# Activations that TensorE holds stationary: the two token halves laid out in turn, and read with a step of two elements

## The chip, the cores and the metric

The kernel runs on one core of a Trainium2 chip. A core has five engines with queues of their own: TensorE (PE, matrix products), VectorE (DVE), ScalarE (ACT), GpSimd (POOL) and SyncE (SP, which issues most transfers). A matrix product on TensorE is two records in the profile: a weight load, which puts a 128x128 stationary block into the array (row PEld), and the matmul proper, which streams a moving block of up to 512 columns past it (row PE). The metric is the device time of one execution in microseconds, lower is better.

## What is computed

One decoder layer on 256 tokens of width 2048, in float32. Cut to the products and what joins them:

```python
proj = x @ w_in                                   # q/k/v/gates of two branches
o = gla_chunked(q, k, v, log_a)                   # gated linear attention, 4 heads
y_gla = o @ w_branch_gla
y_fox = fox_attention(fqh, fkh, fvh, log_f) @ w_branch_fox
mix = (sigmoid(ma) * y_gla + sigmoid(mb) * y_fox) @ w_out
x = layer_norm(ALPHA * x + mix, ln1_g, ln1_b)
h = gelu(causal_dwconv(x @ w_gate, conv_w, conv_b)) * (x @ w_up)
x = layer_norm(ALPHA * x + h @ w_down, ln2_g, ln2_b)
x = x + sigmoid(x @ w_ple_gate) * (p @ w_ple_proj)
```

D_MODEL is 2048 and D_FF 5632, so the weights are 309 MB and each is used once.

## The kernel before

**High and low parts.** Each float32 operand is split into a high part, rounded to the type fp32r by a ScalarE copy, and a low part, the VectorE difference of the operand and its high part. A product is then three fp32r products: high by high, high by low, low by high.

**Which operand is stationary.** There are two kinds of product. In the first (`w_unit` L300, `w_phase` L315) the weights are stationary and the activations move past them, high and low parts of all 256 tokens in one moving block of 512 columns; this serves q, k, the gate and up projections. In the second the activations are stationary, one block of 128 features by 128 tokens at a time, and 512 weight columns move: the value projection (L472), the merge gates and the two branch projections (`q_unit`, L979, called psm, psa and psb), the v and gate projections of the linear attention, the output and down projections and half of the last gate (`s_half`, L841: gv, gr, wo, dn, pg), and the rest (`x_mm`, L353: pg, pp). L909 is the last quarter of pg in 256-column pieces. A block of tokens is one half t of the 256. Every one of these matmuls loads its stationary block anew, also where it is the same as the one before.

**Seven products.** In `s_half` most pairs of weight blocks go through Strassen's scheme, seven products in place of eight. Its sums of activation blocks are made by `s_sums` (L791) on VectorE, split, and kept as cells of 256 columns, high part in columns 0 to 127 and low part in 128 to 255 (`cell`, L787).

**Layout.** An activation tile holds for each block of 128 features a row of 512 columns: the high part of tokens 0 to 127, of tokens 128 to 255, then the low parts in the same order. So a stationary block is always 128 neighbouring columns, `a[:, t * P:t * P + P]`. Tiles of this kind are xT, oT, ofT, mC, x1T, hC, x2T, pTs; mS, xS, hS and gS hold cells. x1T is the only one that is moving alone.

**What sets the order.** Weights arrive in units of 1 MB on SP's queue; `prep` and `prep_s` split them three units ahead of use (L241, L215 with copies at L121). The order on the other engines is set by a scheduler from the order in the code and priorities; TensorE, the bound engine, runs strictly in that order. Some weight differences of the Strassen pairs are made early, parked in memory (POOL's queue) and read back (SP's), both named td.

Of the kernel before, what the change touches and what calls it, by code (L numbers as in the profile page):

```python
# [78 lines left out]
def tile_block(ctx: ExitStack, tc: tile.TileContext, wu, wfv, wpp, xT_in, x_in, pT_in, wlr,  # L79
# [37 lines left out]
    def mxtile(name):  # L117
        return pmx.tile([P, 512], F32, tag="mx", name=name)

# [209 lines left out]
    def comb(ps, o, scale=1.0):  # L329
        tmp = t1("tmp")  # L330
        copy(tmp, ps[:, 256:512], scale)
        a = ps[:, 0:256]
        if len(o.shape) == 3:
            a, tmp = [v.rearrange("p (t n) -> p t n", t=2) for v in (a, tmp)]
# [123 lines left out]
    for u in range(8):  # L458
        hi, lo = fvu[u]
        for j in range(2):  # L460
            kt = 2 * u + j
            a = xT[kt // 4][:, kt % 4, :]
            prods = [[(hi[j], a[:, t * P:t * P + P]), (hi[j], a[:, 256 + t * P:256 + t * P + P]),
                      (lo[j], a[:, t * P:t * P + P])] for t in range(2)]
# [119 lines left out]
    def fox_gen():  # L584
# [40 lines left out]
        def values(h):  # L625
# [7 lines left out]
            copy(dst[:, 0:256], po[:, 0:256])  # L633
            nc.vector.tensor_tensor(dst[:, 256:512], po[:, 0:256],
                                    dst[:, 0:256].bitcast(F32), ALU.subtract)
# [16 lines left out]
    for n in range(16):  # L652
# [8 lines left out]
        comb(ps, fqk[h // 4][:, h % 4, j], (P ** -0.5, 1.0)[j])  # L661
# [137 lines left out]

    def sums(y, name, scale=1.0, full=False):  # L800
# [7 lines left out]
        for e, src in parts:  # L808
            copy(o[:, e, 0:P], src, scale)
            hi = o[:, e, 0:P].bitcast(F32)  # L810
            if scale == 1.0:
                nc.vector.tensor_tensor(o[:, e, P:256], src, hi, ALU.subtract)
            else:
                nc.vector.scalar_tensor_tensor(o[:, e, P:256], src, scale, hi, ALU.mult,
# [111 lines left out]
    def x_sums(pairs):  # L926
        for i, pair in pairs:
# [20 lines left out]
            v = s_sums(y)  # L948
            for j, w in enumerate(ws):
                src = v[:, j * m:j * m + m]  # L950
                copy(w[:, :, 0:P], src)
                nc.vector.tensor_tensor(w[:, :, P:256], src, w[:, :, 0:P].bitcast(F32),
                                        ALU.subtract)
            yield

    def x_cl(pair, j, t):
        kt = 2 * pair + j
        a = xT[kt // 4][:, kt % 4, :]
        return a[:, t * P:t * P + P], a[:, 256 + t * P:256 + t * P + P]

    def x_st(pair, i):
        if i < 3:
            return x_cl(pair, (0, 1, 1)[i], (0, 0, 1)[i])
        o = xS[pair][i - 3]
        return o[:, 0:P], o[:, P:256]


    def q_unit(ps, act, k, first, last, tick=None):
# [4 lines left out]
        def part(i, t):  # L973
            kt = 4 * k + i
            o = act[kt // 4][:, kt % 4, :]
            ah, al = o[:, t * P:t * P + P], o[:, 256 + t * P:256 + t * P + P]
# [139 lines left out]
    def split_T(pt, dst, t):  # L1116

        p3 = pt.rearrange("p (k t) -> p k t", t=P)
        hi = dst[:, :, t * P:t * P + P]
        copy(hi, p3)  # L1120
        nc.vector.tensor_tensor(dst[:, :, 256 + t * P:256 + t * P + P], p3,
                                hi.bitcast(F32), ALU.subtract)
# [19 lines left out]
    def turn_pair(pair):  # L1142
# [19 lines left out]
        nc.vector.scalar_tensor_tensor(dst[:, :, 256:512], p3, 0.5,  # L1162
                                       dst[:, :, 0:256].bitcast(F32), ALU.mult, ALU.subtract)
# [24 lines left out]
    def ln_steps(zof, stats, t, act_out, gb_, cg, cb, nm, prio, aff):  # L1188
# [29 lines left out]
        def turn(g):  # L1218
            zc = zof(t, g)
            with tc.high_priority(prio):  # L1220
# [3 lines left out]
                if g in aff:  # L1224
                    split_T(pt, act_out[g], t)
                    return
                y = t2("lny").rearrange("p (k t) -> p k t", t=P)
                for i in range(4):
# [5 lines left out]
                    else:  # L1234
                        nc.vector.tensor_scalar(y[:, i, :], src, gc, bc, ALU.mult, ALU.add)
                hi = act_out[g][:, :, t * P:t * P + P]
                copy(hi, y)
                nc.vector.tensor_tensor(act_out[g][:, :, 256 + t * P:256 + t * P + P], y,
                                        hi.bitcast(F32), ALU.subtract)
# [3 lines left out]
    def out_proj(nh, tail, mid, end=None):  # L1243
        def cl(pair, j, t):
# [4 lines left out]
            return a[:, t * P:t * P + P], a[:, 256 + t * P:256 + t * P + P]  # L1249
# [170 lines left out]
    for n in range(NF):  # L1420
# [31 lines left out]
        copy(dst[:, 0:256], h)  # L1452
        nc.vector.tensor_tensor(dst[:, 256:512], h, dst[:, 0:256].bitcast(F32), ALU.subtract)
        if pair in DN_S[0] and j == 1:
            v = s_sums(yp)
            for i in range(2):
                w = sm.tile([P, 2, 256], F32R, tag="t2", bufs=6, name="hs")
                copy(w[:, :, 0:P], v[:, 2 * i:2 * i + 2])
                nc.vector.tensor_tensor(w[:, :, P:256], v[:, 2 * i:2 * i + 2],
                                        w[:, :, 0:P].bitcast(F32), ALU.subtract)  # L1460
# [27 lines left out]
    def down(nh, tail, mid):  # L1488
        def cl(pair, j, t):
            a = hC[pair // 2][:, pair % 2 * 2 + j, :]  # L1490
            return a[:, t * P:t * P + P], a[:, 256 + t * P:256 + t * P + P]
# [107 lines left out]
    def g_cl(pair, j, t):  # L1599
        kt = 2 * pair + j  # L1600
        a = x2T[kt // 4][:, kt % 4, :]
        return a[:, t * P:t * P + P], a[:, 256 + t * P:256 + t * P + P]
# [3 lines left out]
    def g_sums(pairs):  # L1606
        two = s8([P, 8, 256], F32R, name=f"gS{pairs[0]}")
        for i, pair in enumerate(pairs):
# [4 lines left out]
            v = s_sums(y)  # L1613
            copy(o[:, :, 0:P], v)
            nc.vector.tensor_tensor(o[:, :, P:256], v, o[:, :, 0:P].bitcast(F32), ALU.subtract)
# [80 lines left out]

def _chan(v):
# [3 lines left out]
def _layout(i):  # L1701
# [26 lines left out]
    for lev in range(1, 8):  # L1728
# [5 lines left out]
    return dict(wu=wu, wfv=wfv, wpp=_xst(i["w_ple_proj"][0]), xT=x.T.reshape(16, P, S).transpose(1, 0, 2),  # L1734
                x=x.reshape(2, P, D), pT=_fold(i["p"][0, 0]).T.reshape(2, P, S).transpose(1, 0, 2),
# [22 lines left out]
```

## Time and profile before

| | before |
|---|---|
| time, median of 3 runs (lowest to highest) | 1645.58 us (1645.08 to 1645.61) |
| span of the profiled execution | 1645.0 us |
| PE, share of the span, matmuls | 1638.4 us, 100%, 8422 |
| PEld, share | 1404.3 us, 85% |
| DVE, share | 1356.0 us, 82% |
| ACT, share | 910.3 us, 55% |
| DMA | 477.81 MB, mean 290 GB/s |
| granted TensorE clock, mean | 1.000 |

The median of the runs is 0.6 us above the span of the profiled execution, so sums made on the span are carried over by adding 0.6. In the chain of waits a row reads: start in us, length in us, engine, tile and line, and how many instructions were merged. Matmuls are pipelined, so the recorded length of one (389 ns for 512 columns) is longer than the distance from one start to the next; the length of a merged row of the chain divided by its count is that distance.

### The profile page before, as it was taken

How to read it: one execution, taken by the hardware profiler on the slowest of the kernel's cores; microseconds unless marked ns; L12 is line 12 of the kernel's file. 1: busy time of each engine (PE TensorE's matmuls, PEld its weight loads, DVE VectorE, ACT ScalarE, POOL GpSimd, SP SyncE). 2: the span in 40 equal slices, each digit the busy share in tenths (PEclk: the TensorE clock that was granted, in tenths of full speed). 3: DMA queues.
4: the chain of work that ended last, by engine and by line, in shares of the span. 5: the costliest groups of instructions: out<-in, count | busy, mean ns of one | idle time of the engine just before them, and what ended most of it. 6: DMA issues, size and time to landing. Idle time of an engine off the chain costs nothing.

```text
span 1645.0 us, 23490 instructions
## 1 busy us (share of the span) xinstructions
PE 1638.4 (100%) x8422; PEld 1404.3 (85%) x8422; DVE 1356.0 (82%) x1964; ACT 910.3 (55%) x1277; POOL 92.7 (6%) x244
## 2 busy tenths in 40 slices
PE   9999999999999999999999999999999999999998
PEld 9988888888888888887898888888888888888887
DVE  7687899788989867778987888887887778988887
ACT  6655555456666654446574445555455456566554
POOL 0000000000000000000010111110111000000000
PEclk9999999999999999999999999999999999999999
DMA  8799799878888768889855898888766679899574
GB/s 324 281 371 341 290 383 356 294 258 309 306 333 307 252 207 303 305 335 364 296 190 194 315 338 320 308 306 304 279 239 217 210 260 336 305 343 348 177 258 157
DMA packets 114838, 477.81 MB, mean 290 GB/s; under 512 B 13032, under 2 KB 14320, under 8 KB 95136
## 3 DMA queue, kind: packets, MB, share of 16 engines
q1 hardware_dynamic: 105216, 417.57, 70.8%
q0 software_dynamic: 9504, 58.73, 8.9%
q8 instruction: 66, 1.08, 0.2%
q14 instruction: 52, 0.43, 0.1%
HBM read 417.53 MB, written 58.73 MB: 290 GB/s over the span
## 4 chain that ended last, share of the span: by engine, by line
PE 97%; DMA 1%; DVE 1%; ACT 0%; issue 0%; POOL 0%; ACTq 0%
PE psm L979 11%; PE dn L841 10%; PE psu L307 10%; PE psg L307 9%; PE psa L979 5%; PE psu L309 5%; PE psg L309 5%; PE dn_p L841 4%; PE gr L841 3%; PE gv L841 3%; PE fv L472 3%; PE pg L353 3%; PE psb L979 3%; PE wo L841 2%; PE gr_p L841 2%; PE gv_p L841 2%
## 5 line engine op out<-in xcount | busy, mean ns | idle before, releaser
L241 DVE TENSOR_TENSOR lo<-raw,hi 128x1024 fp32r<-128x1024 f32 x456 | 551.1, 1220 | 140.7 <-ACT hi L121 139.4
L121 ACT ACTIVATE hi<-raw 128x1024 fp32r<-128x1024 f32 x456 | 476.6, 1057 | 304.2 <-DMA raw<-in_wu_dram 83.7
L307 PE MATMUL psu<-x1T,hi 128*128 128x512 f32 x688 | 240.4, 392 | 0.0
L307 PE MATMUL psg<-x1T,hi 128*128 128x512 f32 x672 | 234.8, 392 | 0.0
L309 PE MATMUL psu<-x1T,lo 128*128 128x256 f32 x688 | 192.3, 280 | 0.0
L309 PE MATMUL psg<-x1T,lo 128*128 128x256 f32 x672 | 187.8, 280 | 0.0
L979 PE MATMUL psm<-hi,xT 128*128 128x512 f32 x512 | 163.0, 392 | 0.0
L307 PEld LDWEIGHTS psu<-x1T,hi 128*128 128x128 f32 x688 | 129.2, 188 | 27.6
L307 PEld LDWEIGHTS psg<-x1T,hi 128*128 128x128 f32 x672 | 126.2, 188 | 27.0
L309 PEld LDWEIGHTS psu<-x1T,lo 128*128 128x128 f32 x688 | 130.6, 190 | 0.0
L121 ACT ACTIVATE hi_b<-raw 128x512 fp32r<-128x512 f32 x112 | 92.9, 841 | 66.8 <-DMA raw<-in_wu_dram 17.9
L309 PEld LDWEIGHTS psg<-x1T,lo 128*128 128x128 f32 x672 | 127.6, 190 | 0.0
L159 DVE TENSOR_TENSOR td<-td 128x512 f32<-128x512 f32 x172 | 117.6, 684 | 0.9
L215 DVE TENSOR_TENSOR lo_b<-raw,hi_b 128x512 fp32r<-128x512 f32 x112 | 104.9, 952 | 15.9 <-ACT hi_b L121 15.6
L979 PEld LDWEIGHTS psm<-hi,xT 128*128 128x128 f32 x512 | 96.2, 188 | 19.6
L215 DVE TENSOR_TENSOR lo_t<-td,hi_t 128x1024 fp32r<-128x1024 f32 x86 | 101.7, 1219 | 12.7 <-ACT hi_t L121 12.0
L121 ACT ACTIVATE hi_t<-td 128x1024 fp32r<-128x1024 f32 x86 | 88.0, 1053 | 28.9 <-DMA td<-td 15.1
L979 PE MATMUL psm<-lo,xT 128*128 128x512 f32 x256 | 99.8, 390 | 0.0
L841 PE MATMUL dn<-hi,hC 128*128 128x512 f32 x352 | 97.8, 389 | 0.0
L979 PE MATMUL psa<-hi,oT 128*128 128x512 f32 x256 | 81.2, 392 | 0.0
L841 PEld LDWEIGHTS dn<-hi,hC 128*128 128x128 f32 x352 | 66.0, 188 | 13.7
L979 PEld LDWEIGHTS psa<-hi,oT 128*128 128x128 f32 x256 | 48.1, 188 | 10.0
(414 smaller groups left out, 3130.8 us busy)
## 6 DMA issues: line engine op xcount, KB each, us to landing
raw<-in_wu_dram SPq DMA_DIRECT2D x525, 512.0 KB, 6.3
td<-in_wu_dram SPq DMA_DIRECT2D x43, 1024.0 KB, 8.8
td<-td POOLq DMA_DIRECT2D x43, 1024.0 KB, 7.7
td<-td SPq DMA_DIRECT2D x43, 1024.0 KB, 8.3
hS<-sd SPq DMA_DIRECT2D x11, 1024.0 KB, 8.8
raw<-in_wu_dram SPq DMA_DIRECT2D x43, 256.0 KB, 7.7
fvraw<-in_wfv_dram SPq DMA_DIRECT2D x13, 524.0 KB, 6.6
sd<-hs POOLq DMA_DIRECT2D x24, 256.0 KB, 5.6
```

What stands on the lines that cost most here:

```text
L121: return nc.scalar.activation(o, i, AF.Copy, bias=0.0, scale=scale)
L159: sub = lambda o, a, b: nc.vector.tensor_tensor(o, a, b, ALU.subtract)
L215: nc.vector.tensor_tensor(lo, src, hi.bitcast(F32), ALU.subtract)
L241: i = nc.vector.tensor_tensor(lo, raw, hi.bitcast(F32), ALU.subtract)
L307: nc.tensor.matmul(ps, lhsT=hi[i // 8 if hoff == 0 else 0][:, w0 % 1024:w0 % 1024 + P], rhs=a[:, kt % 4, :], start=first and i == 0, stop= ...
L309: nc.tensor.matmul(ps[:, 256:512], lhsT=lo[i // 8 if hoff == 0 else 0][:, w0 % 1024:w0 % 1024 + P], rhs=a[:, kt % 4, 0:256], start=False, ...
L353: nc.tensor.matmul(bs[j][:, 0:m], lhsT=x, rhs=v[:, o:o + m], start=first and i == 0, stop=last and i == 2)
L472: nc.tensor.matmul(fbk[t][c][:, 0:n], lhsT=x, rhs=w[:, o:o + n], start=kt == 0 and i == 0, stop=kt == 15 and i == 2)
L841: nc.tensor.matmul(ps[:, e], lhsT=x, rhs=w, start=k == 1, stop=k == total.get(id(ps), 3 * ns))
L979: nc.tensor.matmul(ps[t], lhsT=x, rhs=v, start=first and i == 0 and j == 0, stop=last and i == 3 and j == 2)
```

## The change

The layout of every activation tile that is used stationary changes so that the two blocks of a pair lie in turn. In the high half of a row, column 2n + t holds token n of half t; in the low half likewise. In a cell of a Strassen sum, column 2n + j holds token n of the high part (j = 0) or the low part (j = 1). A stationary block is then 128 columns with a step of two elements. The host lays x and p out this way (`_mix`); on the chip the copies and differences that write such tiles write with a step of two, and the first level of `s_sums` reads with a step of two where its source is laid out so (`mixed`). x1T keeps its layout. The results of q and k of the second branch and of the first come out with tokens in turn, since xT is their moving operand, and `comb` puts them back in order as it reads them. Weight tiles, also those that are stationary, keep theirs. The names of the helpers and the core of the diff:

```diff
+    def tok(a, s, t):
+        return a.rearrange("p (s n t) -> p s t n", s=2, t=2)[:, s, t, :]
+
+    def by_half(v):
+        return v.rearrange("p (n t) -> p t n", t=2)
...
 # x_mm; q_unit, x_cl, g_cl, out_proj and down read the same way
-            ah = a[:, t * P:t * P + P]
-            al = a[:, 256 + t * P:256 + t * P + P]
+            ah, al = tok(a, 0, t), tok(a, 1, t)
...
     def cell(o, i):
-        return o[:, i, 0:P], o[:, i, P:256]
+        v = o[:, i, :].rearrange("p (n j) -> p j n", j=2)
+        return v[:, 0, :], v[:, 1, :]
...
-    def s_sums(y):
-        a11, a21, a12, a22 = [y[:, k, t * P:t * P + P] for k in range(2) for t in range(2)]
+    def s_sums(y, mixed=False):
+        h = y.rearrange("p k (n t) -> p k t n" if mixed else "p k (t n) -> p k t n", t=2)
+        a11, a21, a12, a22 = [h[:, k, t] for k in range(2) for t in range(2)]
...
 # turn_pair, the tile mC: one copy and one difference for two blocks become one of each per block
-        dst = mC[i // 2][:, i % 2 * 2:i % 2 * 2 + 2, :]
-        copy(dst[:, :, 0:256], p3, 0.5)
-        nc.vector.scalar_tensor_tensor(dst[:, :, 256:512], p3, 0.5,
-                                       dst[:, :, 0:256].bitcast(F32), ALU.mult, ALU.subtract)
+        for k in range(2):
+            dst = mC[i // 2][:, i % 2 * 2 + k, :]
+            hi, lo = by_half(dst[:, 0:256]), by_half(dst[:, 256:512])
+            src = p3[:, k, :].rearrange("p (t n) -> p t n", t=2)
+            copy(hi, src, 0.5)
+            nc.vector.scalar_tensor_tensor(lo, src, 0.5, hi.bitcast(F32), ALU.mult, ALU.subtract)
...
 # the gated product of the MLP, tile hC
-        copy(dst[:, 0:256], h)
-        nc.vector.tensor_tensor(dst[:, 256:512], h, dst[:, 0:256].bitcast(F32), ALU.subtract)
+        hi, lo = by_half(dst[:, 0:256]), by_half(dst[:, 256:512])
+        h3 = h.rearrange("p (t n) -> p t n", t=2)
+        copy(hi, h3)
+        nc.vector.tensor_tensor(lo, h3, hi.bitcast(F32), ALU.subtract)
...
+def _mix(a):
+    return a.reshape(-1, 2, P).transpose(0, 2, 1).reshape(a.shape)
...
-    return dict(... xT=x.T.reshape(16, P, S).transpose(1, 0, 2),
+    return dict(... xT=_mix(x.T).reshape(16, P, S).transpose(1, 0, 2),
```

The number and the order of instructions stay as they were on SP and POOL. On TensorE the count stays, and two products change place in the output projection. There VectorE makes the low parts of mC from the transposed blocks mt, among the splits of weights (lo_b, lo_t). Its rows were:

```order
L215 TENSOR_TENSOR lo_b_6992<-raw_1_6982,hi_b_6991 128x1024
L1162 SCALAR_TENSOR_TENSOR mC_6213<-mt_7027,mC_6213 128x2x256
L1162 SCALAR_TENSOR_TENSOR mC_7039<-mt_7034,mC_7039 128x2x256
L215 TENSOR_TENSOR lo_t_6996<-td_6985,hi_t_6995 128x1024
L215 TENSOR_TENSOR lo_t_7000<-td_6985,hi_t_6999 128x1024
```

In the changed kernel they are:

```order
L223 TENSOR_TENSOR lo_b_6994<-raw_1_6984,hi_b_6993 128x1024
L1185 SCALAR_TENSOR_TENSOR mC_6213<-mt_7029,mC_6213 128x2x128
L1185 SCALAR_TENSOR_TENSOR mC_7043<-mt_7038,mC_7043 128x2x128
L223 TENSOR_TENSOR lo_t_6998<-td_6987,hi_t_6997 128x1024
L223 TENSOR_TENSOR lo_t_7002<-td_6987,hi_t_7001 128x1024
L1185 SCALAR_TENSOR_TENSOR mC_6213<-mt_7029,mC_6213 128x2x128
L1185 SCALAR_TENSOR_TENSOR mC_7043<-mt_7038,mC_7043 128x2x128
```

One instruction over 2x256 columns became two over 2x128 for each of the two blocks, and the second of each now stands behind two splits of weights. (A third block, made earlier, and ScalarE's copies for all three are cut in two likewise.) On TensorE, in the first half of the output projection, the two Strassen products whose PSUM banks were mt's (wo_p_7067 and wo_p_7066) stood before:

```order
L841 MATMUL wo_p_6980<-hi_t_6928,mS_6269 128x512
L841 MATMUL wo_p_7067<-hi_t_6928,mS_6269 128x512
L841 MATMUL wo_p_7067<-lo_t_6929,mS_6269 128x512
L841 MATMUL wo_p_7067<-hi_t_6928,mS_6269 128x512
L841 MATMUL wo_p_7066<-hi_t_6932,mS_6269 128x512
L841 MATMUL wo_p_7066<-lo_t_6933,mS_6269 128x512
L841 MATMUL wo_p_7066<-hi_t_6932,mS_6269 128x512
L841 MATMUL wo_10_6977<-hi_t_6932,mS_6269 128x512
```

In the changed kernel they (now wo_p_7073 and wo_p_7072) stand ten matmuls later:

```order
L856 MATMUL wo_01_6978<-hi_b_6993,mS_6551 128x512
L856 MATMUL wo_p_7073<-hi_t_6930,mS_6271 128x512
L856 MATMUL wo_p_7073<-lo_t_6931,mS_6271 128x512
L856 MATMUL wo_p_7073<-hi_t_6930,mS_6271 128x512
L856 MATMUL wo_p_7072<-hi_t_6934,mS_6271 128x512
L856 MATMUL wo_p_7072<-lo_t_6935,mS_6271 128x512
L856 MATMUL wo_p_7072<-hi_t_6934,mS_6271 128x512
L856 MATMUL wo_01_6978<-lo_b_6994,mS_6551 128x512
```

These six matmuls moved from ahead of the next unit's products to among them; nothing else on TensorE moved.

More of the change, by code (lines that the diff above doesn't have):

```diff
@@ L333, in comb @@
         if len(o.shape) == 3:
-            a, tmp = [v.rearrange("p (t n) -> p t n", t=2) for v in (a, tmp)]
+            a, tmp = by_half(a), by_half(tmp)
         if scale == 1.0:
@@ L462, in tile_block @@
             a = xT[kt // 4][:, kt % 4, :]
-            prods = [[(hi[j], a[:, t * P:t * P + P]), (hi[j], a[:, 256 + t * P:256 + t * P + P]),
-                      (lo[j], a[:, t * P:t * P + P])] for t in range(2)]
+            prods = [[(hi[j], tok(a, 0, t)), (hi[j], tok(a, 1, t)), (lo[j], tok(a, 0, t))]
+                     for t in range(2)]
             if u < 2:
@@ L1114, in o_gen, with put_T, split_T @@
             yield
[L1116 to L1122, printed above, removed]
+    def put_T(src, dst, t, mixed):
+        if mixed:
+            hi, lo = [dst.rearrange("p k (s n t) -> p s t k n", s=2, t=2)[:, i, t] for i in range(2)]
+        else:
+            hi, lo = [dst[:, :, o + t * P:o + t * P + P] for o in (0, 256)]
+        copy(hi, src)
+        nc.vector.tensor_tensor(lo, src, hi.bitcast(F32), ALU.subtract)
+    def split_T(pt, dst, t, mixed=True):
+        put_T(pt.rearrange("p (k t) -> p k t", t=P), dst, t, mixed)
     mixers.append(o_gen())
```

66 lines of the change are left out of this document (34 added, 32 removed).

## The prediction

> **What bounds the kernel now.** First the page: the span, the engines, and the shares of the chain of waits.
>
> ```profile
> span 1645.0 us, 23490 instructions
> PE 1638.4 (100%) x8422; PEld 1404.3 (85%) x8422; DVE 1356.0 (82%) x1964; ACT 910.3 (55%) x1277; POOL 92.7 (6%) x244
> PE 97%; DMA 1%; DVE 1%; ACT 0%; issue 0%; POOL 0%; ACTq 0%
> ```
>
> TensorE is busy all the time and 97% of the chain is its own work, so what changes the time must change the distance from one matmul to the next. That distance is read from merged rows of the chain (start in us, length, tile and line, count):
>
> ```profile
> 605.26 21.76 PE psa L979 x96
> 627.02 10.88 PE psb L979 x48
> 1000.09 0.23 PE psg L307
> 1001.13 0.23 PE psg L307
> ```
>
> With activations stationary, 21.76/96 = 10.88/48 = 226.7 ns for 512 columns, steadily. With weights stationary, three pairs of 512 and 256 columns lie between the last two rows: 1.04/3 = 347 ns for 768 columns. What would the array itself need? The early rows, and two later ones, tell:
>
> ```profile
> 3.93 0.85 PE warm_ps L131 x2
> 4.79 1.92 PE fv L472 x6
> 102.41 0.43 PE po L628 x2
> 553.13 0.87 PE gt L1102 x8
> ```
>
> In the first microseconds the array runs at half its rate: 425 ns for 512 columns and 320 ns for 384 columns, 0.83 ns a column in both and nothing fixed on top. Later a column takes half of that, 0.417 ns, so 512 need 213.3 ns and the measured 226.7 has 13.3 ns on top. The pairs have the same: 347 less 768 x 0.417 = 27, for two. So at full rate each matmul pays a fixed 13.3 ns, at half rate none. po (L628) is a product of plain float32 that takes two passes: 215 ns for 256 columns, 0.84 ns a column, and again only some 2 ns on top. So the tax appears where the moving operand is read at full rate: 2048 bytes of each partition in 213 ns, 9.6 bytes a ns. It disappears where the moving operand is read at 4.8 bytes a ns. It belongs to the reading from SBUF, not to the array. The other thing read at that time is the next stationary block. The transposes gt, one load each, follow each other in 0.87/8 = 109 ns, so a load of 128 columns takes at most 109 ns: 512 bytes, 4.7 bytes a ns.
>
> **The change, part by part.** It removes and adds no matmul. It gives each activation block that is loaded a step of two. How many are these? The matmuls of L841, L979, L472, L353 and L909, in this order (span, busy time, count, clock, DMA):
>
> ```profile
> 0.00:1645.00 1645.00, 504.71 (x2214) 1.00 0.80 290
> 0.00:1645.00 1645.00, 312.26 (x1344) 1.00 0.80 290
> 0.00:1645.00 1645.00, 47.20 (x288) 1.00 0.80 290
> 0.00:1645.00 1645.00, 57.86 (x240) 1.00 0.80 290
> 0.00:1645.00 1645.00, 4.81 (x36) 1.00 0.80 290
> ```
>
> Together 4122 of 8422, and 4122 x 13.3 = 54.8 us of tax that the change can touch. No row shows a stationary block with a step, so its price is bounded from both sides. Lower end: the tax vanishes, -54.8 us. Upper end: the step makes it twice as large, +54.8 us (each load then passes over 1024 bytes where it passed over 512). Which is nearer? At full rate the moving operand passes through SBUF at 9.6 bytes a ns and the load at 4.7, so the one overtakes the other during each load; with a step of two the load passes at 9.4 and the two keep their distance. The one row here where both already go equally fast is po, 4.8 against 4.7, and its tax is 2 ns. I take that row: 13.3 - 2 = 11.3 ns less, x 4122 = 46.6 us. The weak point is that in po the reading also has slack, which alone would explain it; the first six fv, at half rate and with slack too, show no tax either.
>
> Not all of the 46.6 us reaches the end, because other work is close behind TensorE in some stages. The value projection, gv, the output projection and the first half of the down projection (length, then busy time of PE, PEld, DVE, ACT, POOL, clock, DMA share and GB/s):
>
> ```profile
> 4.80:50.00 45.20, 45.20 (x280) 44.89 (x280) 30.54 (x36) 27.39 (x37) 3.60 (x6) 1.00 0.92 342
> 365.00:449.00 84.00, 83.91 (x374) 69.18 (x373) 76.56 (x102) 54.47 (x68) 0.00 (x0) 1.00 0.83 296
> 739.00:824.00 85.00, 84.22 (x377) 68.56 (x376) 79.01 (x96) 51.26 (x58) 1.53 (x2) 1.00 0.88 325
> 1318.00:1432.00 114.00, 114.00 (x508) 94.53 (x508) 97.56 (x110) 66.79 (x73) 0.70 (x2) 1.00 0.85 309
> ```
>
> In the output projection VectorE has 79.0 of 85 us and PE already waits; some 360 matmuls would save 4.1 us, and I count none of it. In gv VectorE has 76.6 of 84, so I count half of 4.0. In the value projection the DMA engines are 92% busy, so half of 3.3. Elsewhere, as in the last row (97.6 of 114, against about 108 after), there is room. Given back: 4.1 + 2.0 + 1.6 = 7.7 us.
>
> The rest of the change costs nothing or little. ScalarE and VectorE now write, and in places read, with a step of two. Their price stands in the trace, because L713 works on pieces of runs from 64 elements down to every second element:
>
> ```profile
> L713 ACT ACTIVATE e<-e x28: 399/418/449, 186.9 to 364.5; 128x256 f32<-128x256 f32 x28
> L1437 ACT ACTIVATE yc<-yc 128x256 f32<-128x256 f32 x44 | 18.3, 416 | 54.8 <-DVE yc L1436 54.8
> L718 DVE TENSOR_TENSOR kq<-gk,e x28: 408/416/426, 188.0 to 365.3; 128x256 f32<-128x256 f32 x28
> L1450 DVE TENSOR_TENSOR yp<-yc,up 128x256 f32<-128x256 f32 x24 | 10.1, 422 | 0.7 <-ACT yc L1437 0.2
> ```
>
> All 28 lie in 399 to 449 ns around the 416 ns of an unbroken copy; on VectorE 408 to 426 against 422. So 0, covered in any case by TensorE; without that cover 30 ns on some 150 copies, 4.5 us. The host's reordering is outside the metric; SP's and POOL's transfers keep count, size and order. In the output projection the split of mC into two frees the mt banks later:
>
> ```profile
> 746.51 1.28 DVE L1162 SCALAR_TENSOR_TENSOR mC<-mt,mC 128x512 fp32r<-128x512 f32 x2
> 747.71 2.35 DVE L215 TENSOR_TENSOR lo_t<-td,hi_t 128x1024 fp32r<-128x1024 f32 x2
> 747.46 0.62 PE L841 MATMUL wo_p<-hi_t,mS 128*128 128x512 f32 x2
> ```
>
> The two products that need these banks started at 747.69, and come ten matmuls later now, at 747.69 + 2.27 = 749.96. The second pair of mC stands behind the two lo_t, which end at about 750.0, and takes two times about 0.42. So the first of the products waits until about 750.4: +0.5 us, with the rest of the stage queued behind it on PE.
>
> Sum: 1645.0 - 46.6 + 7.7 + 0.5 = 1606.6 on the profile's span, and with the 0.6 us by which the median exceeds it, 1607 us.
>
> **The rivals.** *The tax is not the load's* (no change). A fixed bubble at the start of each moving stream, which a reader with slack hides and one at full rate cannot, gives the same rows: 13.3 at full rate, none at half. A step in the stationary block then touches nothing but the 0.5 us above: 1646 us. For it: the tax is the same 13.3 ns for blocks of very different addresses. Against it: nothing in the trace, since no full-rate matmul comes without a load beside it. [...]
>
> *Twice the fetches* (slower). If the load reads pieces of several neighbouring columns and each piece stops the moving stream for a moment, a step of two makes twice as many pieces and the tax 26.7 ns: +54.8 us, all on TensorE, 1700 us. It decides from the first matmul and everywhere alike. For it: the tax is there only when the moving reader has no slack, as with stolen turns. Against it: 13.3 ns for a whole load of 109 ns is little for stolen turns.
>
> *The load at half speed* (slower). If two columns come with one read now and one then, a load takes up to 218 ns. The 512-column matmuls still cover it (226.7), but fv, of 384 and 280 columns at 173.3 and 130 ns, and L909, of 256 at 120, would wait for it: 192 x 44.7 + 96 x 88 + 36 x 98 = 20.6 us, 1666 us. Against it: no row of this trace. [...]
>
> **How the numbers follow.** The tax shrinks, 0.55: 1607, with its own range from 1597 (46.6 saved and little given back) to 1630 (half the tax goes, 27.4, less the part lost in the near-bound stages and somewhat more). No change, 0.20: 1645 to 1647. Load at half speed, 0.10: 1666. Twice the fetches, 0.15: 1700. The range 1597 to 1668 leaves out the last rival and some 0.03 of the first case. A measurement here can tell 0.2%, 3.3 us, from no change. Faster 0.55, same 0.20, slower 0.25, from the same cases.
>
> **What would show it.** Right: the rows of psa and psb in the chain at 48 matmuls in about 10.4 us, the psg pairs unchanged at 347 ns, VectorE's share up, waits of PE in the output projection. No tax of the load's: 10.88 again. Twice the fetches: about 11.5. Half speed: 10.88 in psb but the value projection longer by 17 us. The forecast fails if psb stays at 10.88, or if psb falls and new waits of PE on VectorE or DMA take more than the 7.7 us.

## The result, and the profile after

The changed kernel took 1668.99 us (median of 4 runs, 1668.77 to 1669.46), the kernel before 1645.33 us (4 runs, 1644.32 to 1645.61): a ratio of 1.0143, 95% interval 1.0129 to 1.0158. It is slower by 23.7 us where 38.6 us of gain were forecast. The page of the changed kernel, the same three lines as before:

```profile
span 1667.4 us, 23499 instructions
PE 1661.3 (100%) x8422; PEld 1426.3 (86%) x8422; DVE 1359.4 (82%) x1967; ACT 914.3 (55%) x1280; POOL 93.4 (6%) x244
PE 99%; DMA 0%; ACT 0%; DVE 0%; SPq 0%; issue 0%; POOL 0%; POOLq 0%
```

The span grew by 22.4 us, TensorE's busy time by 22.9, and TensorE's share of the chain went from 97 to 99%. No wait was added: the distance between matmuls grew. The chain of waits of the changed kernel shows where (start in us, length in us, tile and line, count):

```profile
614.16 22.40 PE psa L994 x96
636.57 11.20 PE psb L994 x48
...
1003.89 0.12 PE psg L317
...
1005.97 0.12 PE psg L317
```

psb, 48 matmuls in 10.88 us before, takes 11.20: 233.3 ns for 226.7. The tax on 512 columns rose from 13.3 to 20.0 ns. Six pairs of the gate projection lie between the last two rows, 2.08/6 = 347 ns as before: where weights are stationary nothing changed. The down projection moved by the same amount, first before, then after:

```profile
1330.67 6.12 PE dn L841 x27
```

```profile
1344.52 6.30 PE dn L856 x27
```

27 matmuls took 6.12 us (226.7 ns each) and now take 6.30 (233.3). The windows over the whole span for L856, L994, L360, L479 and L924, which answer to L841, L979, L353, L472 and L909 (span, busy time, count, and the same for the loads):

```profile
0.00:1667.40 1667.40, 518.21 (x2214) 428.03 (x2214) 1.00 0.79 287
0.00:1667.40 1667.40, 320.36 (x1344) 257.99 (x1344) 1.00 0.79 287
0.00:1667.40 1667.40, 59.05 (x240) 45.76 (x240) 1.00 0.79 287
0.00:1667.40 1667.40, 46.76 (x288) 46.19 (x288) 1.00 0.79 287
0.00:1667.40 1667.40, 4.82 (x36) 4.61 (x36) 1.00 0.79 287
```

Against the rows of before: 504.71 to 518.21, 312.26 to 320.36, 57.86 to 59.05: together 22.8 us, the whole loss, over 3798 matmuls, 6.0 ns each. The last two, whose streams are 384, 280 and 256 columns, stayed where they were (47.20 to 46.76, 4.81 to 4.82).

So none of the forecast cases came true. The tax neither fell to 2 nor stayed, it did not double to 26.7, and the value projection did not wait for slower loads. A rise by half needs a cause of its own.

### The profile page after: what moved, and what is told of

It is laid out like the page before. It is cut to its first block, busy times and chain, and to the rows that moved or that the text cites. A ratio compares the mean times of both kernels' runs of the same rounds, so it can differ in the third digit from the quotient of the medians.

```text
span 1667.4 us, 23499 instructions
## 1 busy us (share of the span) xinstructions
PE 1661.3 (100%) x8422; PEld 1426.3 (86%) x8422; DVE 1359.4 (82%) x1967; ACT 914.3 (55%) x1280; POOL 93.4 (6%) x244
## 4 chain that ended last, share of the span: by engine, by line
PE 99%; DMA 0%; ACT 0%; DVE 0%; SPq 0%; issue 0%; POOL 0%; POOLq 0%
PE psm L994 11%; PE dn L856 10%; PE psu L315 9%; PE psg L315 9%; PE psa L994 5%; PE psu L317 5%; PE psg L317 5%; PE dn_p L856 4%; PE wo L856 4%; PE gv L856 3%; PE gr L856 3%; PE pg L360 3%; PE psb L994 3%; PE fv L479 2%; PE gr_p L856 2%; PE gv_p L856 2%
## 5 line engine op out<-in xcount | busy, mean ns | idle before, releaser
L994 PE MATMUL psm<-hi,xT 128*128 128x512 f32 x512 | 165.6, 397 | 0.0
L223 DVE TENSOR_TENSOR lo_b<-raw,hi_b 128x512 fp32r<-128x512 f32 x112 | 105.8, 953 | 23.3 <-ACT hi_b L129 22.7
L167 DVE TENSOR_TENSOR td<-td 128x512 f32<-128x512 f32 x172 | 117.7, 685 | 0.9
L994 PEld LDWEIGHTS psm<-hi,xT 128*128 128x128 f32 x512 | 99.0, 193 | 19.7
L994 PE MATMUL psm<-lo,xT 128*128 128x512 f32 x256 | 100.9, 394 | 0.0
L856 PE MATMUL dn<-hi,hC 128*128 128x512 f32 x352 | 100.0, 394 | 0.0
L994 PE MATMUL psa<-hi,oT 128*128 128x512 f32 x256 | 82.6, 397 | 0.0
L856 PEld LDWEIGHTS dn<-hi,hC 128*128 128x128 f32 x352 | 67.9, 193 | 14.1
L994 PEld LDWEIGHTS psa<-hi,oT 128*128 128x128 f32 x256 | 49.6, 194 | 10.0
```

The source lines that it names most:

```text
L167: sub = lambda o, a, b: nc.vector.tensor_tensor(o, a, b, ALU.subtract)
L223: nc.vector.tensor_tensor(lo, src, hi.bitcast(F32), ALU.subtract)
L856: nc.tensor.matmul(ps[:, e], lhsT=x, rhs=w, start=k == 1, stop=k == total.get(id(ps), 3 * ns))
L994: nc.tensor.matmul(ps[t], lhsT=x, rhs=v, start=first and i == 0 and j == 0, stop=last and i == 3 and j == 2)
```

## The experiments

### Series of matmuls alone: the step, the first element, the width, the type

The layer is left out; what is left is this, with a list of series:

```diff
+    def steps(k, a=st):      # 128 columns with a step of k elements
+        v = a[:, 0:D // (P * k) * P * k].rearrange("p (g n k) -> p g k n", k=k, n=P)
+        return lambda i: v[:, i // k % v.shape[1], i % k, :]
+    def series(name, lhs, rhs=one, cols=512, n=48):
+        for i in range(n):
+            nc.tensor.matmul(ps[:, 0:cols], lhsT=lhs(i), rhs=rhs(i), start=i == 0, stop=i == n - 1)
```

> This kernel leaves the whole layer out: it runs only series of 48 matmuls one behind the other, each with its own load, full-rate float32 unless said, 512 columns unless said; the series differ in the step between the 128 columns of the loaded block (1, 2, 3, 4, 8, 16, or 0), in its first element, in the columns streamed (448 to 128), in the step of the streamed operand, and in the type. What is read is the distance between starts less 0.417 ns for each column, the tax: 13.3 ns before the change and 20.0 ns after it. [...] Theory B, bytes that the load passes over: 13.3, 20.0, 26.7 and 33.3 at one to four, but 60 at eight, 113 at sixteen. Theory C, an even or odd place or any step but one: 20.0 at every step above one, and 13.3 against 20.0 for some of the first elements at step one. Theory D, the two operands' steps are compared (equal steps collide): the step of two in the streamed operand turns the order round. [...] Under 256 columns and fewer, where nothing changed in the layer, all steps give one distance.

The chain of waits, one row for each series (start, length, series, count). The letters: s = steps at 512 columns, o = step one from a first element, w = narrower streams (c 384, b 256, a 128), f = plain float32, b = bfloat16:

```profile
23.24 10.88 PE sa_one L59 x48
34.12 11.20 PE sb_two L59 x48
56.62 11.28 PE sc_four L59 x48
67.90 11.76 PE sd_eight L59 x48
79.66 11.35 PE se_sixteen L59 x48
157.66 11.20 PE oe_at_sixteen L59 x48
331.76 8.33 PE wc_one L59 x48
340.09 8.32 PE wc_two L59 x48
407.60 5.31 PE wa_one L59 x48
412.91 5.65 PE wa_two L59 x48
418.56 11.26 PE wa_four L59 x48
443.17 20.60 PE fa_one L59 x48
463.77 20.60 PE fb_two L59 x48
515.33 10.36 PE bb_two L59 x48
```

The series alone repeats the layer to the nanosecond: 10.88/48 = 226.7 ns with step one, 11.20/48 = 233.3 with step two. It refutes theory B: a step of four takes 235.0, of eight 245.0 and of sixteen 236.5, where B said 246.7, 273 and 326. Why eight costs more than sixteen is not shown. The row that decides is `oe_at_sixteen`: adjacent elements, no step at all, but the block begins 16 elements (64 bytes) further on, and it pays 233.3 like a step of two. Streams of 384 columns take 173.4 ns for both steps, bfloat16 215.8 for both (the last row is the step of two). At 448 columns the step of two is even the cheaper one (9.77 us for 48, against 9.91). With streamed operands of step two everything halved its rate (453 ns) and the order did not turn, so theory D falls too. Of theory C the part on places held. Plain float32, the type of po in the prediction, takes 20.60 us for 48 passes of 512 columns at steps of one, two and four alike: 429.2 ns, 2.5 over the 426.7 that the columns need at half rate (0.833 ns each). So po's low tax does not come from the step of its load, and hence not from equal tempo.

Behind 128 columns, 53 ns at 0.417 ns a column, a stream is too short to cover its load, and I read the distance as about the load's own time: 110.6 ns with step one (the transposes of the kernel before stand 109 ns apart), 117.7 with two, 234.6 with four. Of these three steps only four doubles the load. That the load at step two is 7 ns longer does not make the loss: it is covered by 512 columns, which need 213.3 ns.

### Each half of the change undone

Sums plain: the high and low halves of the Strassen sums lie in runs again. Tokens plain: the token halves lie in runs, the halves of the sums in turn.

```diff
 # sums plain (cells and x_st likewise)
-        v = o[:, i, :].rearrange("p (n j) -> p j n", j=2)
-        return v[:, 0, :], v[:, 1, :]
+        return o[:, i, 0:P], o[:, i, P:256]
 # tokens plain (by_half, s_sums, put_T and _mix likewise)
-        return a.rearrange("p (s n t) -> p s t n", s=2, t=2)[:, s, t, :]
+        return a.rearrange("p (s t n) -> p s t n", s=2, t=2)[:, s, t, :]
```

> Half of the change undone: the high and low halves of the seven products' sums lie in runs again, the token halves stay in turn. 792 of the 3798 matmuls of 512 columns with a step of two get a block of adjacent elements back. If each such matmul pays by itself for its own block's step (5.8 ns each): 1669.0 - 4.6 = 1664.4 us. If blocks of different kinds behind one another pay as well (each kind's own phase), the gain is under half of that: 1667 or more. If the sums' halves make the whole loss (a split operand written in turn, read again by VectorE): 1646.

> The other half undone: the token halves lie in runs again (and the inputs' columns in their old order), the halves of the sums stay in turn. 3006 matmuls of 512 columns get adjacent elements back, 792 keep the step of two. By 5.8 to 6.1 ns for each matmul: 1669.0 - 17.7 = 1651.3 us, 6 over the kernel before (with 792 x 5.8 = 4.6 of it in the sums' products). If blocks of different kinds pay as well: 1655 or more. If the sums' halves make the whole loss: 1669.

Measured: 1665.03 us (ratio to the kernel before 1.0116, 1.0101 to 1.0131) and 1650.66 us (1.0029, 1.0018 to 1.0039), for 1664.4 and 1651.3 expected. In the chain of waits of the first, then of the second, dn_p are products of sums and most of dn products of token blocks:

```profile
1350.27 2.04 PE dn_p L854 x9
1352.31 6.30 PE dn L854 x27
```

```profile
1341.76 2.10 PE dn_p L856 x9
1343.86 6.12 PE dn L856 x27
```

2.04/9 and 6.12/27 are 226.7 ns, 2.10/9 and 6.30/27 are 233.3. Each product pays for its own block, whichever stands beside it, and the two halves add up. Against the kernel before as it ran beside them (1646.20 us), the two are 18.8 and 4.5 us slower, together 23.3 us, where the whole change costs 23.7. What is left for the copies, the differences and the reading in turn cannot be told from nothing.

### Series alone: where the two operands begin

```diff
+    for o in places:
+        series(f"a_{o}", at(o))                   # the loaded block begins at o
+    for o in places:
+        series(f"c_{o}", at(0), w5(o))            # the streamed operand begins at o
+    for o in (8, 16, 32, 48):
+        series(f"d_{o}", at(o), w5(o))            # both
```

> Again only series of matmuls, 32 each, with the whole layer left out. The first series showed that a loaded block with step one at the offsets 0 and 64 (elements of 4 bytes) pays 13.3 ns over the columns of 512, but 19 to 20 ns at the offsets 4, 8, 16 and 32, and that blocks with a step of four hold the next start back to 233 ns even behind 128 columns. Names: a = step one from the offset in the name; b = step two from that offset; c = step one at 0, the streamed operand moved by the offset; d = both moved; e = step two, the streamed operand moved; f = 64 or 32 columns loaded; g = streams of 256 to 504 columns; h = streams of 512 and 256 columns in turn under one block, at step one and at step two; z = the first one again. Theory A, only the distance between the two operands' first addresses counts (a phase between two readers): d_8 to d_48 pay 13.3 again, c pays like a at the mirrored offset, and for some offset b or e returns to 13.3. Theory B, only the loaded block's own place within 256 bytes counts: c pays 13.3 throughout, d pays like a, and b and e stay at 20.0 or over. Theory C, the load's length against the stream counts: f pays less than 13.3, and b 20.0 at every offset. If the pair under one block pays for a step of two, h_2 is 353 to 360 ns a pair against 347 for h_1; otherwise both are 347. A series below 13.3 would name an arrangement that is faster than the kernel before.

Pieces of the chain of waits from inside six series: a at 0, a at 16, a at 48, c at 16, c at 48, d at 16:

```profile
28.18 6.80 PE a L59 x30
50.28 6.77 PE a L59 x29
80.13 6.64 PE a L59 x29
265.58 6.64 PE c L59 x29
280.58 6.53 PE c L59 x28
324.59 6.37 PE d L59 x28
```

That is 226.7, 233.4, 229.0, 229.0, 233.2 and 227.5 ns. Moving the stream by 16 is the same as moving the block by 48 (229.0 twice), moving it by 48 the same as moving the block by 16, and moving both by 16 gives nearly all of it back. The mean distances of more series, from the starts in the trace (ns, offsets in elements):

```
offset                       0      8      16     32     48     64
block moved, step one      226.7  233.4  233.4  232.3  228.9  227.0
stream moved, step one     226.7  233.3  228.9  232.4  233.3  227.1
both moved, step one       226.7  227.5  227.5  228.0  228.0
block moved, step two      235.6  232.2  230.1  231.5  233.4  233.3
```

The 235.6 is the one value of the table that did not repeat: the same series took 233.3 in the next experiment. The highest value with adjacent elements was 234.2, at 24. Theory A holds in the main: the distance between the two first addresses sets the tax, and it repeats after 64 elements, 256 bytes, within 0.4 ns at six of the seven places that were repeated (the seventh, 60 and 124, took 228.3 and 226.7). The place itself counts for about 1 ns: moving both operands together gives 14.2 to 14.7 ns of tax, not 13.3. Loads of 64 or 32 columns still took 230.1 and 231.7 ns, so the load's length is not it (theory C). No series of 512 columns lies under 226.7: the layer before had the best distance of those tried. Pairs of 512 and 256 columns under a block with step two took 350.1 ns against 353.1 with step one: for them the step is not even dearer.

### The distance, tried in the layer

Both kernels leave some columns of SBUF unused between the pools of the weights and of the activations (line 36). One number moves every activation by 64 bytes against the weights and changes nothing else:

```diff
-GAPS = (96, 64, 80)
+GAPS = (96, 80, 80)
```

> The kernel before with one number changed: the unused columns between the pools of the weights and the pools of the activations are 80 and not 64, so every activation lies 64 bytes further on against the weights; no step of two anywhere. If what a product of 512 columns pays depends on the distance between the first addresses of its loaded block and of its stream (phase theory), the series with a step of one and 16 elements of distance say 233.4 ns for 226.7 behind 3798 loaded activation blocks, +22 to +25 us, and 228.9 ns for the 1872 products of the gate and up projections whose block is a weight (16 elements the other way), +4 us: 1670 to 1675, slower than the changed kernel although no block has a step. If the step of the block is what costs, by itself: 1646, no change.

> The changed kernel with the same 64 bytes. Phase theory: in the series a step of two at 16 elements of distance took 230.1 ns for 233.3 at none, so the 3798 products get back 3.2 ns each, -12 us, and the gate and up products pay 2.2 ns for 1872 of them, +4 us: about 1661, now faster than the kernel before with the same shift. If the step costs by itself: 1669, no change. If a shift costs every product of full rate alike: 1680 or more.

The kernel before with the shift: 1659.39 us, ratio 1.0102 (1.0069 to 1.0136); three of its four executions took 1658.5 to 1659.6 us, one 1671.16. The changed kernel with it: 1655.53 us, ratio to the kernel before 1.0058 (1.0034 to 1.0083). The kernel before, shifted, in its chain of waits:

```profile
635.30 11.20 PE psb L979 x48
...
1101.09 0.23 PE psg L307
...
1102.11 0.23 PE psg L307
```

psb takes 11.20 us, exactly as in the changed kernel, and no block has a step. The changed kernel, shifted:

```profile
1381.65 6.21 PE dn L856 x27
```

6.21/27 = 230.0 ns, the 230.1 that the series gave for a step of two at a distance of 16, for 233.3 without the shift. Both products moved as the distance said, one up and one down. That the step itself costs is refuted as the whole explanation.

The times were off all the same: the shifted kernel before took 1659.39 us where 1670 to 1675 were expected, and it is not slower than the changed kernel. The reason is a term that I had with the wrong sign. I expected the pairs where weights are stationary to lose 2.2 ns; three of them lie between the last two rows of the shifted kernel before, 1.02/3 = 340.0 ns for 347. Over its whole span the 1872 pairs (gate, up, queries and keys) average 343.5 ns for 347.9, -8 us. The profiled execution of the changed, shifted kernel has the pairs at 349.1. Its ten executions fall into two groups, 1649.2 to 1650.8 and 1660.3 to 1662.5 us, five each, and the chain shows why:

```profile
860.96 0.23 PE psu L315
...
861.98 0.23 PE psu L315
...
1100.98 0.23 PE psg L315
...
1102.03 0.23 PE psu L315
```

Three pairs in 1.02 us, 340 ns, near 861 us; three in 1.05, 350 ns, near 1101. The pairs have two rhythms at this distance, and an execution can change from one to the other on its way. By the starts in the trace this one changes once, at 950 us, right behind a wait of TensorE for a low part (0.76 us idle). From there on 1087 pairs run at 350 ns, 10.9 us more than at 340, which is about the distance of the two groups. A wait alone does not do it: the shifted kernel before has one of the same length near 955 us and stays at 340.0 to its last pair.

### Series alone: steps of two at all places, and narrower streams

> Series of 32 matmuls alone, the layer left out. First a step of two at 32 first elements from 0 to 124 in fours, then at six odd ones, then two blocks with a step of two in turn (the even and the odd elements of one stretch, as the kernel reads them) at eight places, a step of four at four places, and 256 columns streamed with step one and step two at four places. Phase theory: the distances with step two repeat after 64 elements, lie between 229 and 236 ns with a lowest place near 16, odd and even first elements within 1 ns of one another, no place at 226.7. If some place is at 226.7 or below, the change could be had without its loss. 256 columns: 120 at every place if they are covered by the load's own time, or up to 6 ns more at 16 and 32 if the phase counts there as well.

The chain of waits: step two from 16 (7.37/32 = 230.3 with the change of series in it); then 256 columns with adjacent elements, the stream moved by 48:

```profile
59.15 7.37 PE bae__286 L59 x32
...
413.13 3.63 PE c__1952 L59 x32
```

Over all 32 places the step of two took 230.0 to 233.9 ns and repeated after 64 elements to 0.1 ns; odd places equalled the even ones just below (233.3 at 1, 230.0 at 17). None of the places reaches 226.7, so no first element that was tried gives the change without a loss. The 256 columns were a surprise: not 120 or more, but 113.4 ns with the stream 48 elements on. So under these narrower streams 6.7 ns (113.4 less 106.7 for the columns) is the least tax measured, not 13.3, and there may be better distances than those of the kernel before.

### Pairs in turn, and a kernel from it

> Series alone, the layer left out; every loaded block of adjacent elements. First pairs as in the gate and up projections: a block from one tile behind 512 columns, a block from a second tile behind the first 256 of them, 18 pairs for each of 64 combinations of the two blocks' offsets (0 to 56 in eights). Then 512 columns twice in turn with two offsets, 36 combinations. In the layer a pair takes 347.9 ns before the change (231 + 117) and 343.5 ns where the activations lie 64 bytes further on. Theory A (a phase between the two operands that carries over from one matmul to the next): the 64 combinations differ by 10 ns or more, the one that stands for the layer (0, 16) near 348, the shifted one (48, 0) near 343.5, and the lowest lies under both. Theory B (each matmul pays for its own distance alone): a pair is the sum of what the single series gave for its two distances, (0, 16) 226.7 + 113.3 = 340. For the twins: by A some combination of two unlike offsets may lie under 226.7; by B none does, the mean of two singles is the twin's.

The 64 combinations took 345 to 354 ns, (0, 16) 346.7, (48, 0) 350.0; the sum of two single series, 340, was not reached by (0, 16). So theory B falls: something carries over from matmul to matmul, as theory A has it. A's figures were only half met: the spread is 9 ns where it asked for 10, and (48, 0) was to be near 343.5. Of 36 combinations of two 512-column products none lay under 226.6. The layer's 340.0 at the shifted distance did not show, so its distances were tried in the layer itself:

```diff
-LO_SHIFT = 16
+HI_SHIFT = 112
...
-        o = 0 if any(u in r for r in UA) else LO_SHIFT
-        return rlo.tile([P, 1152], F32R, tag="lo", name=f"lo{name}")[:, o:o + 1024]
+        return rlo.tile([P, 1024], F32R, tag="lo", name=f"lo{name}")
+    def hi_tile(u, name):
+        o = 0 if any(u in r for r in UA) else HI_SHIFT
+        return rhi.tile([P, 1152], F32R, tag="hi", name=f"hi{name}")[:, o:o + 1024]
```

UA are the units of weights that stream past activations; the others are loaded as blocks.

> The kernel before, no step of two; only the weights that are themselves loaded as blocks (query and key, gate, up) lie otherwise: their high halves 112 elements into a slot of 1152, their low halves at the slot's start and no longer 16 elements into it. Their distances to the activations, modulo 512 bytes, are then those of the run with 64 more unused bytes, where the 1872 pairs of the gate and up projections took 343.5 ns for 347.9; the activations that are loaded as blocks keep their distance and their 226.7 ns. Phase theory: 1645.5 - 1872 x 4.4 ns = 1637.3 us, faster than both kernels; in executions that fall into the other rhythm (349.1 ns a pair, as in the changed kernel with the same shift) about 1647.5. If the gain of the pairs in that run came from the products around them and not from their own distances: 1645.5.

> Series alone, the layer left out: pairs of 512 and 256 columns as before, but 40 for each of 64 combinations of the two blocks' offsets from 0 to 112 in sixteens, so that offsets count modulo 512 bytes. If 512 bytes are the period, (48, 64), the distances of the shifted run, gives 343.5 and (64, 80), those of the kernel before, 347.9, unlike the (48, 0) and (0, 16) of the series before (350.0, 346.7). If 256 bytes are the period, the table repeats its 4 by 4 corner within 1 ns. If the rhythm depends on where a series happens to begin, the two halves of one series or the repeats of the corner differ by several ns.

The kernel: 1636.89 us, ratio to the kernel before 0.9969 (0.9948 to 0.9989). It has two groups too, five executions at 1634.9 to 1636.9 and four at 1645.8 to 1647.2, near the 1637.3 and 1647.5 that were expected. The median belongs to the first group; an execution of the second is no faster than the kernel before (1645.28 us). Its profiled execution is of the second group:

```profile
625.99 10.88 PE psb L982 x48
```

psb keeps its 226.7 ns. The pairs run at 340 ns from 856 us on and at 350 from 939 us to the end, again 1087 of them. Here the change comes at the first pair of a new tile, and the trace shows no long wait before it. There is no profile of an execution of the first group. The series at the same time, windows over 40 pairs at (48, 0) and at (48, 64):

```profile
364.29:377.89 13.60, 13.60 (x82) 12.03 (x81) 0.00 (x0) 0.60 (x1) 0.00 (x0) 1.00 0.00 1
419.76:433.76 14.00, 14.00 (x82) 12.27 (x81) 0.00 (x0) 0.60 (x1) 0.00 (x0) 1.00 0.00 1
```

Here (48, 0) keeps 340 ns and (48, 64), the layer's distances, 350, over the whole series. Of the 16 places of the corner, 14 repeat at 64 elements within 0.5 ns. The other two do not: (48, 0) and (112, 0) took 340.0, (48, 64) and (112, 64) 350.0, the layer's two rhythms, and (48, 16) took 346.7 or 353.3 in the same way. So at some distances the rhythm depends on how a series begins, as the last reading of the expectation has it. (16, 0) took 340 in all four of its repeats, which looked like a place with one rhythm.

### The place with one rhythm, in the layer; and threes

```diff
-HI_SHIFT = 112
+HI_SHIFT = 16
```

> As the run with the high halves of the weights 112 elements into their slots, but 16 elements: the high half's distance is then 16 modulo 64 elements and the low half's 0. In the series of pairs (16, 0), (16, 64), (80, 0) and (80, 64) took 340.0 ns in both halves of the series, while (48, 0) and (112, 0) took 340.0 but (48, 64) and (112, 64) 350.0; the run with 112 lay at these and fell into the one rhythm in some executions and into the other in the rest. By the phase theory every execution now runs its pairs at 340.0 for 346.7 to 347.9: 1645.3 - 1872 x 6.7 to 7.9 ns = 1630.5 to 1632.8 us, with a spread of 2 us at most. If the rhythm is set by what runs ahead of the pairs and not by the distances, it stays in two groups near 1636 and 1647.

> Series alone, the layer left out: three products of 512 columns in turn as where activations are loaded: a block x a stream, the same block x a second stream, a second block x the first stream; the second block is 0 to 112 elements off in sixteens, the second stream as well, 14 threes for each of 64 combinations, all with adjacent elements. With no offsets 3 x 226.7 = 680.0 ns. If 32 cycles are the least that such a product pays, no combination lies under 680. If a rhythm with 16 cycles for some of the three exists, as the pairs have (340.0 for 512 + 256 columns, 48 cycles over their columns for two), some combination lies at 673 or 667, and a kernel faster again could be had.

The kernel took 1654.69 us, ratio 1.0048 (1.0035 to 1.0061): slower, not faster. Five of its six executions lie between 1654.1 and 1655.4 and one at 1651.1, so there is no second group 10 us away; but the rhythm is a bad one:

```profile
1100.93 0.23 PE psu L310
...
1101.99 0.23 PE psu L310
```

Three pairs in 1.06 us, 353 ns, where 340 was expected. The first series of pairs had run the same place, (16, 0), at 353.3 ns. Below are its window of 18 pairs and that of 40 pairs from the second series:

```profile
130.01:136.37 6.36, 6.36 (x39) 5.53 (x38) 0.00 (x0) 0.60 (x1) 0.00 (x0) 1.00 0.00 0
140.87:154.48 13.62, 13.62 (x82) 12.07 (x81) 0.00 (x0) 0.60 (x1) 0.00 (x0) 1.00 0.00 1
```

6.36/18 = 353.3 ns and 13.62/40 = 340.5: this place has two rhythms as well, and the layer's profiled execution took the slow one. Within a series the rhythm stays as it began, and the two series differ in what ran ahead of this place and in the number of pairs. So something beside the two distances sets it, and what that is stays open. Of the threes, none of 64 combinations took less than 680.0 ns, three times 226.7 (the expectation's 32 cycles are the 13.3 ns of tax in units of 0.417 ns, the time of one column); the rest took up to 700.0. For products that load activations the kernel before stands at the best of all distances that were tried.

## Why the prediction was wrong

**What bounds the kernel** was right: TensorE alone. The growth of three lines' busy time, 22.8 us, is about the growth of the span, 22.4.

**The count** was too large by 324. Streams of 384 and 256 columns paid nothing for the step, in the layer and in the series (8.33 and 8.32 us). The 3798 of 512 columns carry it all.

**The step that failed** is the choice between the two ends: "with a step of two the load passes at 9.4 and the two keep their distance. The one row here where both already go equally fast is po [...] I take that row." With equal tempo the series pays 20.0 ns, not 2, so tempo does not take the tax away. What the runs show in its place is that the tax of these products depends on the step and on where the two operands begin against one another, modulo 256 bytes: without any step, 64 bytes of distance bring the same 20.0 in the series and in the layer. At the distance that the kernel has, adjacent elements pay the least of all places tried, 13.3; a step of two pays 20.0 there, and 16.7 at its best place. So -46.6 us became +22.8. Why the step costs 6.7 ns, by which resource, stays open. That po's low tax may come from slack was named as the weak point, and the runs bear it out: in plain float32 the tax is 2.5 ns at steps of one, two and four alike (20.60 us for 48), so equal tempo is not what makes it low. The series of bfloat16, which read half as many bytes for each column, have 2.5 ns at every step too. That slack is the reason fits both, but no run varies it alone.

**The rivals.** "The tax is not the load's" was half right: the base of 13.3 ns did not vanish in any arrangement of 512 columns of this type, and 64 or 32 loaded columns did not lower it; but the part above it depends on the load's address. In bfloat16 2.5 ns are left between streams (10.36 us for 48, 215.8 ns each); in the type of this kernel the place of one reading shows in the time of the other: 226.7 to 234.2 ns with adjacent elements, by the distance of the two. "Twice the fetches" had the right sign and the wrong law: the tax did not double (20.0, not 26.7), and steps of four, eight and sixteen paid 21.7, 31.7 and 23.1 ns, in no order of the fetches. "The load at half speed" is what a step of four does (234.6 ns); at two the load takes 117.7, and nothing waited.

**The range** ended at 1668, just under the result. The two ends of the cost, -54.8 and +54.8 us, held it; what was missing was a rival that raises the tax by a part of itself, so that all the weight on the slow side lay at +20.6 and +54.8 us with another mechanism behind each.

**What was given back and what hid.** The 7.7 us could not be tested, since nothing was saved. The slack behind it shows from the other side. The output projection, in the window that answers to the prediction's third row:

```profile
751.00:836.60 85.60, 85.60 (x374) 71.46 (x373) 78.51 (x97) 50.70 (x59) 1.53 (x2) 1.00 0.87 324
```

85.00/377 = 225.5 ns a matmul became 85.60/374 = 228.9, +3.4 where other stages have +6. The rest came out of waits: TensorE was busy for 84.22 of 85.00 us in the prediction's row and for all of the 85.60 here. The split of mC cost 0.1 us where 0.5 were expected:

```profile
762.98 1.51 PE wo_p L856 x6
```

Six products in 1.51 us are 0.11 more than six times 233.3 ns. The copies that now write in turn, before and after:

```profile
L121 ACT ACTIVATE hC<-yp 128x256 fp32r<-128x256 f32 x24 | 9.9, 411 | 8.5 <-DVE yp L1450 8.5
```

```profile
L129 ACT ACTIVATE hC<-yp 128x256 fp32r<-128x256 f32 x24 | 10.3, 430 | 8.1 <-DVE yp L1469 8.1
```

19 ns more on ScalarE, where 0 was taken and 30 named as the price without cover. It was covered, as said.

## What to carry to other kernels

When two operands are read at the same time at the full rate, look at where they begin against one another before looking at steps: here 64 bytes of distance cost a matmul as much as the change did, 6.7 ns, and that edit changes only addresses. A series of some 30 matmuls for each distance gave the price of single products, nearly always to a few tenths of a ns, and it carried over to the layer (230.1 and 230.0 ns). For products of unlike lengths in turn it did not, so those have to be timed in place, and more than once: an earlier series that disagrees is a warning. A bound that is only a doubling and a vanishing deserves a case between them, and a row that is chosen for one property (equal tempo) and has a second one (slack) is no evidence for the first.

## What the runs showed of the hardware that I had not expected

- A full-rate float32 (fp32r) matmul of 512 columns followed the next at 226.7 to 234.2 ns by the distance of its two operands' first addresses, with a period of 256 bytes and adjacent elements in both; moving both together changed it by no more than 1.3 ns. In bfloat16 it was 215.8 at steps of one, two, four and eight of the loaded block.
- 256 columns took 113.4 to 120 ns by the same distance, so 13.3 ns is no fixed price: 6.7 was seen there, though never for 512 columns.
- Pairs of 512 and 256 columns can run in two stable rhythms, 340.0 and 350.0 ns, at one and the same distance, and an execution can change from one to the other on its way. The 1087 pairs behind such a change make 10.9 us; two groups of times 10 to 12 us apart appeared at a granted clock of 1.00.
- Behind streams of 128 columns one matmul followed the next at 110.6, 117.7 and 234.6 ns with steps of one, two and four float32 elements in the loaded block, which I read as the load's own time, and a streamed operand with a step of two halved the matmul's rate (453 ns for 512 columns).
- Which resource lies behind the dependence on the distance is not shown by any run here.
